# Encoder block on one core: a re-ordered front and a re-timed attention plan

## The chip, the cores and the metric

The kernel runs on one core of a Trainium2 chip. Five engines work side by side, each through its own queue in order: TensorE (PE in the profile; its weight loads are PEld), VectorE (DVE), ScalarE (ACT), GpSimd (POOL) and SyncE (SP), which issues nearly all DMAs. The metric is the device time of one execution in microseconds (us); the time of the kernel before is the median of three executions.

## The reference, cut to what matters

One encoder block on 512 tokens, preceded by 16 meta tokens (528 columns in all), with a model width of 1024.

```python
u = rms_norm(h, pre_mix_gain)
qa, ka, va, qb, kb, vb, g = split(u @ w_in)
qa, ka, qb, kb = (rope(t, pos) for t in (qa, ka, qb, kb))
o_swa = windowed_gqa_sink_attention(qa, ka, va, sink)       # 16 query heads on 4 key heads, width 64
lam = exp(sum(lq1 * lk1)) - exp(sum(lq2 * lk2)) + lambda_init
o_diff = differential_attention(qb, kb, vb, lam)            # 8 heads: (softmax(q1 k1) - lam softmax(q2 k2)) v
merged = sigmoid(g1) * (o_swa @ w_swa) + sigmoid(g2) * (o_diff @ w_diff)
h = h + rms_norm(merged @ w_out, post_mix_gain)
u = rms_norm(h, pre_ffn_gain)
h = h + rms_norm((silu(u @ w_gate) * (u @ w_up)) @ w_ffn_out, post_ffn_gain)
```

## The kernel before, in words

**Arithmetic.** Every operand of a large product is split into a high part (rounded to fp32r) and a low remainder, and a product is three matmuls, high by high, high by low, low by high (mm3, lines 286 to 288). ScalarE makes the high part, VectorE or GpSimd the low one (split at L256, sub_hi at L252). A weight tile is 128 x 1024 (0.5 MB): a raw tile "wr" (three buffers) is loaded, then split into "wh" and "wl" (three each). x is transposed in memory and kept as xh and xl, eight chunks of 128 rows by 528 columns, scaled by the norm's gain; the norm's own factor for each token, rbc, is multiplied in only after the products.

**The front** (L364 to about L500) is written out by hand. DVE, ACT and SP take its instructions in the order of the program, inside a block called start; PE takes the whole kernel so. In order:

- 60 warm-up matmuls on a zero tile (L377).
- The loads: vec (small vectors, the gain among them), chunk 0 of x, the first half of the two key weights wA and wB, the rest of x, the second halves after chunk 2. x_load and x_split (L388 to L395) load and split a chunk of x, w_half (L397 to L403) half a weight tile. Then load_w loads and splits wV (the first value weight) and wV2 (the second); its cast is L271. Then come the four tiles xn of plain x, xm (the meta tokens), ident and rot (the table of the rotation).
- The key products: for each of the eight chunks k, and for wA and wB, and for both halves of the 528 columns (HALF is 264), one mm3. Then the product of wV, into two banks pV.
- The norm: sums of squares of the five tiles, on ACT (L454, three of them) and DVE (L456, two). After them ACT copies the key sums out of PSUM (kraw, L461 and L462). rsqrt_cols makes the inverse root (POOL and DVE), and PE turns it into a row by five transposes (L468 and L471); ACT copies it into rbc (L472, L473).
- lambda: a DMA of its vectors into lt (L481), two reductions on DVE (L485), an exponential on ACT (L487), and two operations on DVE that leave -lambda in nlam (L488, L489).
- two masks and a zeroed tile.

**The attention plan.** From L502 the kernel does not issue instructions directly: it makes a list of some 2,580 tasks, each with an engine, an assumed cost, what it reads and writes, which ring of buffers it takes a place from, a priority, and for a DMA (land) how long the data takes after the issue. Plan.run (L175) goes through them like a small model of the chip, when the kernel is built: at each step it takes, of the engines' next possible tasks, the one that can start first; of those within 0.12 us of each other on one engine, the one with the earliest due time. For PE the due time is the priority itself, for the other engines the time at which the task is ready plus SLACK of its priority. The order that comes out is the fixed order of each engine's queue on the chip; the modelled times are not used there.

In the plan: the two value products of the windowed attention (v_swa; that of wV2 is made in the plan, by products, from the splits that the front made), transposed by PE after a scaling by rbc on DVE into VT (L581; transposes at L591 and L599); the rotation of the keys, copied by SP into place (move, L569); four groups of queries (q_swa, two weight tiles each, 512 columns), 16 blocks of windowed attention (s_swa, products at L706; t_swa, transposes at L755, products at L762 and L765); gate products; eight heads of differential attention (qk, vd, s_diff with products at L854, t_diff with products at L894 to L909); and branch products that fill in between. weights() loads and splits a weight tile for all of them (cast at L522); odd ones get their low part from POOL, even ones from DVE. s_diff multiplies by nlam for each head's second softmax (L872). Tag "vt" has one buffer, for VT.

The plan ends near 500 us. The second branch, the output product, the norm and the feed-forward part (to 951 us) follow in hand-written order.

Of the kernel before, what the change touches and what calls it, by code (L numbers as in the profile page):

```python
# [20 lines left out]
P = 128  # L21
# [94 lines left out]
class Plan:  # L116
# [6 lines left out]
    AFTER = dict(PE=0.22, ACT=0.07, DVE=0.07, POOL=0.12, SP=0.1)  # L123

    def __init__(self, tags):
        self.slots = {t: [0.0] * n for t, n in tags.items()}
        self.tasks, self.sigs, self.bufs, self.last = [], {}, [], {}
# [47 lines left out]
    def run(self):  # L175
        free = dict.fromkeys(("PE", "ACT", "DVE", "POOL", "SP"), 0.0)
# [3 lines left out]
        while any(todo.values()):  # L180
            best = None
            for e, ks in todo.items():
                cand = []
                for k in ks:
                    t = 0.0
                    for d in k.deps:
                        if d.done is None:
                            t = None
                            break
                        t = max(t, d.done + (0.0 if d.eng == e else self.AFTER[d.eng]))  # L190
# [5 lines left out]
                    for tag, n in need.items():  # L196
# [4 lines left out]
                        t = max(t, f[n - 1] + 0.07)  # L201
# [3 lines left out]
                    due = k.prio if e == "PE" else t + self.SLACK.get(k.prio, 6.0 + 0.002 * k.prio)  # L205
                    cand.append((max(t, free[e], port if k.port else 0.0), due, k))
# [18 lines left out]
            free[k.eng] = t + k.cost  # L225
            k.done = t + k.cost + k.land
            if k.port:
                port = t + k.cost
            k.fn()
            for b in k.bufs:  # L230
                b.left -= 1
                if not b.left and b.tag is not None:
                    self.slots[b.tag][b.slot] = max(u.done + (0.0 if u.eng == "PE" else 0.0) for u in b.users)
# [3 lines left out]
def encoder(ctx, tc, I, out, dbg=None):  # L237
# [209 lines left out]

    ss = const.tile([P, 5], F32, name="ss")
# [9 lines left out]
    kraw = [atp.tile([P, EXT], F32, tag="q", name="kraw", bufs=8) for _ in range(2)]  # L458
    for s in range(2):
        cs = slice(s * HALF, (s + 1) * HALF)  # L460
        act.copy(out=kraw[0][:, cs], in_=kA[s])  # L461
        act.copy(out=kraw[1][:, cs], in_=kB[s])  # L462
# [8 lines left out]
    pe.transpose(out=Sw[1][:, 0:P], in_=rb, identity=ident)  # L471
    act.copy(out=rbc[:, NMETA:EXT], in_=rps)  # L472
# [6 lines left out]

    lt = atp.tile([P, 4, 64], F32, tag="rt", name="lt", bufs=RT)  # L480
    sp.dma_start(out=lt, in_=I["lam"])  # L481
    lj = atp.tile([P, 2, 64], F32, tag="rt", name="lj", bufs=RT)
    ls = const.tile([P, 2], F32, name="ls")
    for c in range(2):
        dve.tensor_tensor_reduce(out=lj[:, c], in0=lt[:, 2 * c], in1=lt[:, 2 * c + 1], scale=1.0,  # L485
                                 scalar=0.0, op0=ALU.mult, op1=ALU.add, accum_out=ls[:, c:c + 1])
    act.activation(out=ls, in_=ls, func=AF.Exp)  # L487
    dve.tensor_tensor(out=nlam, in0=ls[:, 1:2], in1=ls[:, 0:1], op=ALU.subtract)  # L488
# [1097 lines left out]
```

## Time and profile before

| | |
|---|---|
| median of 3 runs | 949.91 us (949.45 to 951.23) |
| the profiled execution | 952.51 us |
| its span, first to last instruction | 950.7 us |
| TensorE busy | 932.1 us (98%) |
| VectorE, ScalarE, GpSimd busy | 716.5, 525.3, 216.7 us |
| mean granted TensorE clock | 0.996 |
| bytes moved by DMA | 110.46 MB, 116 GB/s in the mean |

The profile is of one execution. Times count from its first instruction. Rows of a timeline give the start, the duration, the engine, the line of the kernel, the operation, what it writes and reads, and in brackets how long the engine was idle before it and what released it. A row of the table by stretches gives the stretch, its length, the busy time and number of instructions of PE, PEld, DVE, ACT and POOL, the granted clock (1.00 is full), the DMA engines' busy share and GB/s. Rows of the groups give the line, the operation, its tiles and shape, the count, the busy time, the mean ns of one and the idle time before them. Rows of the waits give who waited for whom, the sum, how often, and the longest. The rows of the DMA issues end in the KB of each and the median us from issue to landing. Matmuls overlap in the array, so their durations add up to more than the time between their starts.

### The profile page before, as it was taken

The numbers are of one execution on the slowest core, as the hardware profiler recorded it, in microseconds if no ns is written. First come the engines' busy times: TensorE is split into PE (matmuls) and PEld (weight loads), VectorE is DVE, ScalarE is ACT, GpSimd is POOL, SyncE is SP. The second block draws the span as 40 slices with busy tenths as digits, with TensorE's granted clock in tenths as the row PEclk, the third lists the DMA queues.
The fourth block names the chain that finished last, engine by engine and source line by source line (L and its number), as shares of the span: only waits on it lengthen the run. The fifth ranks groups of instructions, "written<-read, shape, count | busy, mean of one in ns | idle before, by whom it ended". The sixth has DMA issues, their size and how long they took to land.

```text
span 950.7 us, 15639 instructions
## 1 busy us (share of the span) xinstructions
PE 932.1 (98%) x5871; PEld 833.9 (88%) x5871; DVE 716.5 (75%) x1230; ACT 525.3 (55%) x954; POOL 216.7 (23%) x228
## 2 busy tenths in 40 slices
PE   9899999999999999999999999999999999999996
PEld 9787888889898999989887888998999999988885
DVE  5747898999664658878773865885787887799975
ACT  6326776775644446667556443563555555565541
POOL 0544455543222423243211421400000000000000
PEclk9999999999999999999999999999999999999999
DMA  9483222251535144333531470354433333180122
GB/s 333 132 216 100 68 78 73 73 135 45 135 89 144 58 113 134 82 107 127 157 111 55 162 223 26 91 189 143 116 107 96 115 101 111 46 332 16 52 67 88
DMA packets 37579, 110.46 MB, mean 116 GB/s; under 512 B 6129, under 2 KB 6641, under 8 KB 37505
## 3 DMA queue, kind: packets, MB, share of 16 engines
q1 hardware_dynamic: 37504, 109.47, 38.4%
q8 instruction: 46, 0.75, 0.3%
q14 instruction: 29, 0.23, 0.1%
HBM read 88.09 MB, written 2.10 MB: 95 GB/s over the span
## 4 chain that ended last, share of the span: by engine, by line
PE 85%; DMA 5%; DVE 4%; ACT 2%; SPq 2%; issue 1%; POOL 1%; DVEq 0%; POOLq 0%; ACTq 0%
PE pr L286 19%; PE pr L288 19%; PE pr L287 19%; PE Sd L854 3%; PE wk L287 2%; PE wk L286 2%; PE wk L288 2%; PE Sw L706 2%; PE O L762 2%; PE tr L894 2%; PE Od L907 2%; DMA wr<-in_w_in_dram 2%; PE tr L755 2%; PE tr L287 1%; PE tr L288 1%; PE tr L286 1%
## 5 line engine op out<-in xcount | busy, mean ns | idle before, releaser
L286 PE MATMUL pr<-xh,wh 128*128 128x264 f32 (+1 forms) x616 | 200.6, 326 | 0.0
L287 PE MATMUL pr<-xl,wh 128*128 128x264 f32 (+1 forms) x616 | 196.9, 320 | 0.8 <-DVE xl L394 0.8
L288 PE MATMUL pr<-xh,wl 128*128 128x264 f32 (+1 forms) x616 | 196.8, 319 | 0.3 <-POOL wl L252 0.3
L252 POOL TENSOR_TENSOR wl<-wr,wh 128x1024 fp32r<-128x1024 f32 (+2 forms) x42 | 100.0, 2382 | 142.0 <-ACT wh L522 78.8
L288 PEld LDWEIGHTS pr<-xh,wl 128*128 128x128 f32 x616 | 116.3, 189 | 9.0 <-POOL wl L252 0.5
L287 PEld LDWEIGHTS pr<-xl,wh 128*128 128x128 f32 x616 | 116.5, 189 | 8.8 <-DVE xl L394 1.2
L286 PEld LDWEIGHTS pr<-xh,wh 128*128 128x128 f32 x616 | 116.2, 189 | 7.7 <-issue 0.2
L522 ACT CAST wh<-wr 128x1024 fp32r<-128x1024 f32 x56 | 58.5, 1048 | 45.0 <-PE pr L287 29.7
L252 DVE TENSOR_TENSOR wl<-wr,wh 128x1024 fp32r<-128x1024 f32 (+2 forms) x58 | 67.9, 1174 | 17.4 <-ACT wh L271 8.5
L308 POOL TENSOR_TENSOR r3y<-r3v,mhalf 128x1 f32<-128x1 f32 x4 | 2.2, 551 | 326.9 <-DVE r3v L307 326.9
L286 PE MATMUL pr<-TM,sx 128*128 128x256 f32 x236 | 66.9, 283 | 0.3 <-ACT s L1368 0.3
L287 PE MATMUL pr<-TM,sx 128*128 128x256 f32 x236 | 66.8, 283 | 0.0
L288 PE MATMUL pr<-TM,sx 128*128 128x256 f32 x236 | 66.8, 283 | 0.0
L859 DVE TENSOR_REDUCE nm<-Sd 128x1 f32<-128x528 f32 x64 | 45.1, 705 | 20.8 <-PE Sd L854 19.9
L252 DVE TENSOR_TENSOR sx<-S,sx 128x1024 fp32r<-128x1024 f32 x34 | 41.6, 1225 | 25.1 <-PE pr L287 12.7
L288 PE MATMUL pr<-uh,wl 128*128 128x256 f32 (+1 forms) x188 | 55.0, 292 | 0.4 <-DVE wl L252 0.4
L286 PE MATMUL pr<-uh,wh 128*128 128x256 f32 (+1 forms) x188 | 55.1, 293 | 0.0
L287 PE MATMUL pr<-ul,wh 128*128 128x256 f32 (+1 forms) x188 | 54.9, 292 | 0.0
L559 POOL TENSOR_TENSOR ta<-ta,tb 128x528 f32<-128x528 f32 (+1 forms) x26 | 36.4, 1400 | 79.8 <-DVE tb L547 53.9
L256 ACT CAST sx<-S 128x1024 fp32r<-128x1024 f32 x34 | 35.7, 1050 | 25.5 <-PE pr L288 9.2
L862 ACT ACTIVATE pp<-Sd,nm 128x528 f32<-128x528 f32 x40 | 28.0, 700 | 39.3 <-DVE pa L875 22.6
L720 POOL TENSOR_SCALAR p<-p,rc 128x272 f32<-128x272 f32 (+1 forms) x64 | 36.1, 577 | 48.4 <-DVE rc L718 45.1
(522 smaller groups left out, 2641.6 us busy)
## 6 DMA issues: line engine op xcount, KB each, us to landing
wr<-in_w_in_dram SPq DMA_DIRECT2D x50, 512.0 KB, 4.4
wg<-in_w_fi_dram SPq DMA_DIRECT2D x17, 512.0 KB, 3.6
wu<-in_w_fi_dram SPq DMA_DIRECT2D x17, 512.0 KB, 3.5
wr<-in_w_fi_dram SPq DMA_DIRECT2D x16, 512.0 KB, 4.3
b<-in_w_fo_dram SPq DMA_DIRECT2D x16, 512.0 KB, 8.7
Kd<-hl SPq DMA_DIRECT2D x32, 132.0 KB, 2.4
Kd<-Kd SPq DMA_DIRECT2D x16, 264.0 KB, 3.9
Q<-hl SPq DMA_DIRECT2D x64, 64.0 KB, 3.1
```

What stands on the lines that cost most here:

```text
L252: (eng or dve).tensor_tensor(out=lo, in0=src, in1=hi.bitcast(F32), op=ALU.subtract)
L256: act.copy(out=hi, in_=src)
L286: pe.matmul(out=ps, lhsT=ah, rhs=bh, start=first, stop=False, **more)
L287: pe.matmul(out=ps, lhsT=ah, rhs=bl, start=False, stop=False, **more)
L288: pe.matmul(out=ps, lhsT=al, rhs=bh, start=False, stop=last, **more)
L522: T("ACT", 1.05, lambda: act.copy(out=wh.t, in_=wr.t), r=[wr], w=[wh], prio=pr_)
L559: T("POOL", 0.05 + 1.3 * m, lambda: pool.tensor_tensor(out=ta.t[:, :, 0:n], in0=ta.t[:, :, 0:n], in1=tb.t[:, :, 0:n], op=ALU.add), r=[tb], ...
L706: pe.matmul(out=Sw2[S.slot][:, 0:nk], lhsT=QS[g][hh].t[:, i * P:(i + 1) * P], rhs=KB[g].t[:, x, r0:r1], start=(x == 0), stop=(x == 1))
L720: T("POOL", 0.2 + 0.43 * c, lambda z=z: pool.tensor_scalar(out=pt.t[:, z, 0:nk], in0=pt.t[:, z, 0:nk], scalar1=rc.t[:, z:z + 1], scalar2=1 ...
L854: pe.matmul(out=S.t[:, s, 0:HALF], lhsT=Q[c].t[:, i * P:(i + 1) * P], rhs=K[c].t[:, x, s * HALF:(s + 1) * HALF], start=(x == 0), stop=(x = ...
L859: T("DVE", 0.71, lambda S=S, c=c, one=one: dve.tensor_reduce(out=nm.t[:, c, one], in_=S.t[:, :, 0:HALF], axis=AX.XY, op=ALU.min), r=[S], w ...
L862: T("ACT", 0.9, lambda S=S, c=c, one=one, p=p: act.activation(out=p().rearrange("p (a b) -> p a b", a=2), in_=S.t[:, :, 0:HALF], func=AF.E ...
```

## The change

Four things are changed; the matmuls, their shapes and their number stay.

**First operands.** x chunk 0 is loaded first, then vec. The weight tiles wA and wB come in three pieces instead of two halves: chunks 0 and 1 after x chunk 0, chunks 2 and 3 after x chunk 1, chunks 4 to 7 after x chunk 3. In the key products of chunk 0 the twelve matmuls are put in another order: the four high by high first, then the four with xl, then the four with wl.

**Second V product.** wV2 is loaded and split after xn and xm instead of before them. The kraw copies move from behind the last sum of squares to behind the first. The product of wV2 is made in the front, in two banks of "pr": the first four chunks of its first half before the five transposes of the norm, the rest after them. The plan no longer holds it.

**lambda** moves into the plan as tasks, its DMA after the transposes of block 5, with lt in the "vt" buffer; the DVE multiply by nlam waits for it.

**The planner.** Its engines' ends, signal delays and costs are replaced by other figures, the engines start at given times (PE at 3.7), and the due times of 206 tasks are moved by the amounts of a list (SHIFT).

```diff
-    AFTER = dict(PE=0.22, ACT=0.07, DVE=0.07, POOL=0.12, SP=0.1)
+    OVER = dict(PE=0.0, ACT=0.098, DVE=0.083, POOL=0.03, SP=0.0)
+    DRAIN = dict(PE=0.165, ACT=0.0, DVE=0.0, POOL=0.0, SP=0.0)
+    def lag(a, b):
+        return 0.07 if b == "PE" else 0.06 if b == "SP" else 0.092 if b == "POOL" and a in ("ACT", "DVE") else 0.036
+    SHIFT = """
+        28:20 51:-25 66:6.4 98:5 111:6 146:7 155:8 175:-5 184:17 198:-4.3 216:-89 218:-15 222:-6 257:-68 266:0.7
...
+        2579:48"""
...
-                        t = max(t, d.done + (0.0 if d.eng == e else self.AFTER[d.eng]))
+                        t = max(t, d.start + d.cost if d.eng == e == "PE" else d.done + self.lag(d.eng, e))
...
                     due = k.prio if e == "PE" else t + self.SLACK.get(k.prio, 6.0 + 0.002 * k.prio)
+                    due += self.shift.get(k.n, 0.0)
...
-            free[k.eng] = t + k.cost
-            k.done = t + k.cost + k.land
+            free[k.eng] = t + max(0.06, k.cost - self.OVER[k.eng]) if k.eng != "PE" else t + k.cost
+            k.done = t + k.cost + k.land + self.DRAIN[k.eng]
...
-    x_load(0)
-    w_half(wA, 0, 0)
-    x_split(0)
-    w_half(wB, 1, 0)
-    for k in range(1, KT):
+    for k in range(KT):
         x_load(k)
         x_split(k)
-        if k == 2:
-            w_half(wA, 0, 1)
-            w_half(wB, 1, 1)
+        for k0, k1 in {0: ((0, 2),), 1: ((2, 4),), 3: ((4, KT),)}.get(k, ()):
+            w_part(wA, 0, k0, k1)
+            w_part(wB, 1, k0, k1)
     wA, wB = wA[1:], wB[1:]
     wV = load_w(I["w_in"][2], dst=[atp.tile([P, KT, P], F32R, tag="p", name="wV", bufs=2) for _ in range(2)])
-    wV2 = load_w(I["w_in"][3])
     for t in range(4):
         sp.dma_start(out=xn[:, t], in_=I["x"][t * P:(t + 1) * P])
     sp.dma_start(out=xm, in_=I["meta"])
+    wV2 = load_w(I["w_in"][3])
...
     for k in range(KT):
...
+        todo = [(ps_, w[a][:, k, :], (xh, xl)[b][:, k, cs], k == 0 and a == b == 0, k == KT - 1 and a == 1)
+                for hs, w in ((kA, wA), (kB, wB)) for ps_, cs in zip(hs, halves) for a, b in ((0, 0), (0, 1), (1, 0))]
+        if k == 0:
+            todo = [x for p in range(3) for x in todo[p::3]]
+        for ps_, a, b, first, last in todo:
+            pe.matmul(out=ps_, lhsT=a, rhs=b, start=first, stop=last)
...
+        if t == 0:
+            for ps_, raw in ((kA, kraw[0]), (kB, kraw[1])):
+                for s in range(2):
+                    act.copy(out=raw[:, halves[s]], in_=ps_[s])
+    pV2 = [pr_t(HALF), pr_t(HALF)]
+    def v2(h, ks):
+        for k in ks:
+            mm3(pV2[h], (wV2[0][:, k, :], wV2[1][:, k, :]), (xh[:, k, halves[h]], xl[:, k, halves[h]]), k == 0, k == KT - 1)
+    v2(0, range(KT // 2))
     rst = rsqrt_cols(const, ss, P, 1.0 / D, "r0")
...
     pe.transpose(out=Sw[1][:, 0:P], in_=rb, identity=ident)
+    v2(0, range(KT // 2, KT))
+    v2(1, range(KT))
...
-                   ta=2, tb=1, vt=1, rt=RT, ma=3))
+                   ta=2, tb=1, vt=1, rt=RT, ma=3), dict(PE=3.7, ACT=0.05, DVE=0.05, POOL=0.0, SP=0.0))
...
-          w=[wr], dep=dep, prio=pr_, land=3.6 if nfill[0] > 3 else 0.3)
+          w=[wr], dep=dep, prio=pr_, land=4.0 if nfill[0] > 3 else 0.0)
...
-            T("PE", 3 * mm_t(c1 - c0),
+            T("PE", 0.694 if c1 - c0 == NTOK else 0.367,
...
-    def move(out, in_, r, w, dep=(), land=2.7):
+    def move(out, in_, r, w, dep=(), land=2.3):
...
+    def lam_task():
+        lt = sb("vt", [P, 4, 64], F32, "lt", 1)
+        T("SP", 0.35, lambda: sp.dma_start(out=lt.t, in_=I["lam"]), w=[lt], dep=Ttr[5][-1:], prio=60, land=3.0)
...
-    v_swa([products(w3, X, X_, h * HALF, (h + 1) * HALF) for h in range(2)])
+    v_swa(PV2)
```

The other costs of the plan are changed in the same way, by up to a few tenths of a microsecond each (a transposition of four blocks from 0.50 to 0.355, an exponential of a differential head from 0.90 to 0.79, a low part on POOL from 2.65 to 2.42).

More of the change, by code (lines that the diff above doesn't have):

```diff
@@ L175, in run @@
     def run(self):
-        free = dict.fromkeys(("PE", "ACT", "DVE", "POOL", "SP"), 0.0)
+        free = self.free
         port = 0.0
@@ L232, in run @@
                 if not b.left and b.tag is not None:
-                    self.slots[b.tag][b.slot] = max(u.done + (0.0 if u.eng == "PE" else 0.0) for u in b.users)
+                    self.slots[b.tag][b.slot] = max(u.done for u in b.users)
         self.end = max(k.done for k in self.tasks)
@@ L445, in encoder @@
         proj(pV[h], wV, X, h * HALF, (h + 1) * HALF)
+    kraw = [atp.tile([P, EXT], F32, tag="q", name="kraw", bufs=8) for _ in range(2)]
     ss = const.tile([P, 5], F32, name="ss")
@@ L478, in encoder @@
     pool.tensor_scalar(out=g08, in0=vec[:, 40:41], scalar1=1.0 - LAMBDA_INIT, scalar2=1.0, op0=ALU.mult, op1=ALU.mult)
[L480 to L488, printed above, removed]
-    dve.tensor_scalar(out=nlam, in0=nlam, scalar1=-LAMBDA_INIT, scalar2=None, op0=ALU.add)
     bd1 = atp.tile([P, 512], F32R, tag="rt", name="bdm", bufs=RT)
@@ L572, in encoder @@
     X_ = []
-    w3 = [pl.held(t, x) for t, x in zip(("wh", "wl"), wV2)]
+    for t in ("wh", "wl"):
+        pl.slots[t][0] = 3.9
     def v_scaled(pv):
@@ L639, in encoder @@
     PV = [pl.held("tr", t) for t in pV]
+    PV2 = [pl.held("pr", t) for t in pV2]
     for b in MK:
@@ L696, in s_swa @@
         sm = [buf() for _ in range(2)]
-        T("POOL", 0.27, lambda: pool.tensor_copy(out=pt.t[:, :, nk], in_=nsink[:, 4 * g:4 * g + 4]),
+        T("POOL", 0.2, lambda: pool.tensor_copy(out=pt.t[:, :, nk], in_=nsink[:, 4 * g:4 * g + 4]),
           w=[pt] + ph, prio=0)
@@ L811, in qk @@
                      [hl], [K])
-            move(lambda K=K: K.t[64:128], lambda K=K: K.t[0:64], [], [K], land=4.0)
+            move(lambda K=K: K.t[64:128], lambda K=K: K.t[0:64], [], [K], land=3.6)
             for i in range(2):
@@ L861, in s_diff @@
                   prio=0)
-                T("ACT", 0.9, lambda S=S, c=c, one=one, p=p: act.activation(
+                T("ACT", 0.79, lambda S=S, c=c, one=one, p=p: act.activation(
                     out=p().rearrange("p (a b) -> p a b", a=2), in_=S.t[:, :, 0:HALF], func=AF.Exp, scale=-1.0,
@@ L867, in s_diff @@
                 if c == 0:
-                    T("POOL", 0.78, lambda p=p, one=one: pool.tensor_scalar(
+                    T("POOL", 0.715, lambda p=p, one=one: pool.tensor_scalar(
                         out=p(), in0=p(), scalar1=rc.t[:, 0, one], scalar2=1.0, op0=ALU.mult, op1=ALU.mult),
@@ L878, in s_diff @@
         hd["a"], hd["A"], hd["keep"] = a, A, [pa, pp[0]]
+    def lam_task():
+        lt = sb("vt", [P, 4, 64], F32, "lt", 1)
+        ls = const.tile([P, 2], F32, name="ls")
+        T("SP", 0.35, lambda: sp.dma_start(out=lt.t, in_=I["lam"]), w=[lt], dep=Ttr[5][-1:], prio=60, land=3.0)
+        LS = buf()
+        for c in range(2):
+            T("DVE", 0.23, lambda c=c: dve.tensor_tensor_reduce(
+                out=lt.t[:, 2 * c], in0=lt.t[:, 2 * c], in1=lt.t[:, 2 * c + 1], scale=1.0, scalar=0.0, op0=ALU.mult,
+                op1=ALU.add, accum_out=ls[:, c:c + 1]), w=[lt, LS], prio=7, port=True)
+        T("ACT", 0.2, lambda: act.activation(out=ls, in_=ls, func=AF.Exp), w=[LS], prio=7)
+        T("DVE", 0.16, lambda: dve.tensor_tensor(out=nlam, in0=ls[:, 1:2], in1=ls[:, 0:1], op=ALU.subtract),
+          w=[LS], prio=7)
+        T("DVE", 0.16, lambda: dve.tensor_scalar(out=nlam, in0=nlam, scalar1=-LAMBDA_INIT, scalar2=None, op0=ALU.add),
+          w=[LS], sig="lam", prio=7)
     lnx, dd, results, B1 = [], [], [], []
@@ L898, in t_diff @@
                 T("ACT", 0.58, lambda: act.copy(out=aTm[32:48, :], in_=tr.t[0:16, :]), r=[tr], w=[AM], prio=1)
-                hd["Av"].append(T("PE", mm_t(512), lambda: pe.matmul(out=O.t, lhsT=m.t, rhs=aTm, start=False, stop=True),
+                hd["Av"].append(T("PE", 0.232, lambda: pe.matmul(out=O.t, lhsT=m.t, rhs=aTm, start=False, stop=True),
                                   r=[AM, m], w=[O], prio=0))
@@ L990, in encoder @@
         T("ACT", 0.36, lambda c=c: act.copy(out=aTm[:, c * 256:(c + 1) * 256], in_=zero), w=[AM], prio=2)
+    lam_task()
     qk(0)
```

75 lines of the change are left out of this document (35 added, 40 removed), and 15 rows, old and new, of the table SHIFT.

## The prediction

> **What bounds the kernel now.** I read the page first, then the table by stretches of time, then TensorE's own waits, then the timelines around them.
>
> ```profile
> span 950.7 us, 15639 instructions
> ...
> PE 932.1 (98%) x5871; PEld 833.9 (88%) x5871; DVE 716.5 (75%) x1230; ACT 525.3 (55%) x954; POOL 216.7 (23%) x228
> ...
> PE 85%; DMA 5%; DVE 4%; ACT 2%; SPq 2%; issue 1%; POOL 1%; DVEq 0%; POOLq 0%; ACTq 0%
> ```
>
> ```profile
> 6.00:24.90 18.90, 18.07 (x146) 17.50 (x144) 12.66 (x19) 13.07 (x22) 0.61 (x1) 1.00 1.03 392
> 24.90:35.10 10.20, 8.98 (x67) 8.15 (x65) 7.93 (x20) 3.88 (x8) 5.80 (x7) 1.00 0.45 142
> 35.10:38.50 3.40, 1.06 (x7) 0.50 (x5) 3.37 (x8) 1.54 (x3) 2.38 (x2) 1.00 0.13 51
> 38.50:42.00 3.50, 3.50 (x11) 2.72 (x10) 3.10 (x4) 1.11 (x3) 3.50 (x3) 0.51 0.05 4
> 42.00:500.00 458.00, 453.69 (x2826) 400.70 (x2826) 344.60 (x742) 271.43 (x576) 167.26 (x177) 1.00 0.40 108
> ```
>
> TensorE is busy 98% of the span and carries 85% of the chain, so time is won only where it waits. Behind each stretch and its length stand the busy times of PE, PEld, DVE, ACT and POOL, then the granted clock, the DMA share and GB/s. The change touches only what lies before 500 us, and the matmuls stay the same in number. PE idles 1.22 us in 24.9 to 35.1, 2.34 in 35.1 to 38.5, and 4.31 in 42 to 500, where the attention plan rules; at 38.5 to 42 it is busy, but at clock 0.51.
>
> Busy time hides small waits, because matmuls overlap:
>
> ```profile
> 232.56 0.28 PE L287 MATMUL pr<-xl,wh 128*128 128x264 f32 x1
> 232.69 0.28 PE L288 MATMUL pr<-xh,wl 128*128 128x264 f32 x1
> 233.68 0.39 PE L854 MATMUL Sd<-Kd,Qd 128*128 128x264 f32 x1 [0.72 <-ACT pp L862]
> ...
> 506.27 0.40 PE L286 MATMUL pr<-xh,wh 128*128 128x512 f32 x1
> 506.50 0.40 PE L287 MATMUL pr<-xl,wh 128*128 128x512 f32 x1
> ```
>
> A 264-wide matmul reads 0.28 us but is followed after 0.12; a 512-wide one reads 0.40 and is followed after 0.23. The wait shown as 0.72 really cost 0.99 - 0.12 = 0.87, and waits under 0.16 are not shown at all. So I count the plan's work by shape:
>
> ```profile
> L286 PE MATMUL pr<-xh,wh 128*128 128x264 f32 x384 | 111.2, 290 | 0.0
> ...
> L286 PE MATMUL pr<-xh,wh 128*128 128x512 f32 x172 | 68.8, 400 | 0.0
> ...
> L854 PE MATMUL Sd<-Kd,Qd 128*128 128x264 f32 x256 | 43.3, 291 | 1.0 <-ACT pp L862 0.7
> ...
> L921 PE MATMUL mp<-sh,ones 128*128 128x512 f32 x7 | 2.8, 394 | 0.0
> ```
>
> In 42 to 500 there are 3 x 384 + 256 = 1408 matmuls of 264 columns (L287 and L288 are like L286) and, from the x172 row to the x7 row, 918 of 512. At 0.121 and 0.2325 that is 170 + 213 us. The other 500 of the 2826 (64 of 400 columns, 64 of 272, 372 transposes of 128) I put at 0.155 and 0.09, between those spacings and below: 53 us. Together 436 of 458, so about 22 us go into waits, of which the profile shows 4.3.
>
> **The change part by part.** The sum is made on the profiled execution, 952.51 us (span 950.7 and 1.8 around it), 2.6 above the median of 949.91; I carry the gain over to the median.
>
> *First operands.* The warm-up matmuls end where real work begins:
>
> ```profile
> 0.97 5.14 PE L377 MATMUL wps<-warm 128*128 128x128 bf16 x60 [0.97 <-DVE warm L374]
> ...
> 5.92 0.37 PE L286 MATMUL pr<-xh,wh 128*128 128x264 f32 x1
> ...
> 6.71 0.39 PE L287 MATMUL pr<-xl,wh 128*128 128x264 f32 x1 [0.42 <-DVE xl L394]
> ...
> 8.27 0.39 PE L286 MATMUL pr<-xh,wh 128*128 128x264 f32 x1
> ...
> 9.08 0.39 PE L287 MATMUL pr<-xl,wh 128*128 128x264 f32 x1 [0.41 <-DVE xl L394]
> ```
>
> They stay, so nothing starts before 5.9. What can go is 6.71 - 5.92 - 0.12 = 0.67 and 0.69 the second time. For k = 0 the four high-by-high matmuls now come first and cover the making of xl and wl: the first stall goes. The second, on x of k = 1 and 2, shrinks by little, because the loads run at a full DMA share (1.03 in 6 to 24.9). I take 0.8, between 0 and 1.4.
>
> *The norm chain.* This is where I expect the price of the new front.
>
> ```profile
> 16.67 1.05 ACT L271 CAST wh<-wr 128x1024 fp32r<-128x1024 f32 x1
> 18.01 1.06 ACT L454 ACTIVATE jk<-xn 128x1024 bf16<-128x1024 f32 x1 [0.29 <-DMA xn<-in_x_dram]
> ...
> 22.85 1.06 ACT L454 ACTIVATE jk<-xm 16x1024 bf16<-16x1024 f32 x1 [0.73 <-DMA xm<-in_meta_dram]
> 23.81 0.18 ACT L454 ACTIVATION_READ_ACCUMULATOR jk<-xm 16x1 f32 x1
> 23.91 0.35 ACT L461 COPY kraw<-pr 128x264 f32<-128x264 f32 x1
> ...
> 26.44 0.69 PE L468 MATMUL rps<-ident,rb 128*128 128x128 f32 x4 [1.21 <-issue]
> ```
>
> On ScalarE this part runs in program order: the kraw copies stand behind the last Square although their sums were long ready. The second V weight's cast (L271) still stands ahead of the first Square, but its 0.5 MB now queues behind xn and xm. With the DMA engines full, the same bytes are ahead of its end as of xm's end now, so I put its landing at 22.3 (xm's is 22.8; x now leads the queue, half a microsecond sooner). Then follow one cast, a Square, four kraw copies of 0.35 that overlap a little, two Squares: 22.3 + 1.0 + 1.1 + 1.1 + 1.15 + 1.15 = about 27.6. VectorE's subtraction and two reductions run beside them. From the last accumulator read (23.99) to the first transpose (26.44) it takes 2.45 us, so that comes at 30.0, 3.5 later. The 12 V2 matmuls put ahead as filler last 12 x 0.12 = 1.45 and wait for the first kraw copy (24.8): TensorE idles from 26.3 to 30.0, 3.7 us where it idles 1.4 now. Bounds: no delay if the weight lands as early as the first xn (18.0), 4 us if it trails xm.
>
> *The clock.* In the stretch 35.1 to 38.5 TensorE worked 1.06 us, and the stretch after it was granted 0.51:
>
> ```profile
> 36.16 0.33 PE L599 MATMUL tr<-ident,VT 128*128 128x128 f32 x1 [0.69 <-DVE VT L581]
> 38.14 0.57 PE L599 MATMUL tr<-ident,VT 128*128 128x128 f32 x3 [1.65 <-DVE VT L581]
> 38.44 0.70 PE L286 MATMUL pr<-xh,wh 128*128 128x512 f32 x1
> 38.94 0.63 PE L287 MATMUL pr<-xl,wh 128*128 128x512 f32 x1
> 39.36 0.63 PE L288 MATMUL pr<-xh,wl 128*128 128x512 f32 x1
> ...
> 42.06 0.40 PE L288 MATMUL pr<-xh,wl 128*128 128x512 f32 x1
> ```
>
> Matmuls came 0.42 apart instead of 0.23; nine of them from 38.44 to 42.29 lost 1.7 us. My new idle of 3.7 should bring the same, partly over idle time: 1.2, between 0 and 1.7. [...]
>
> *Second V product and lambda.* Those two VT waits (and the lost clock) go, since V2 is done before the plan and VectorE is rid of lambda ahead of it:
>
> ```profile
> 30.92 1.78 DVE L485 CUSTOM_DVE_ANT_0 lj<-lt 128x64 f32<-128x64 f32 x1 [0.57 <-DMA lt<-in_lam_dram]
> ...
> 36.03 0.91 DVE L488 TENSOR_TENSOR nlam<-ls 128x1 f32<-128x1 f32 x1
> ```
>
> Moved into the plan, lambda is one DMA issue on SP after the transposes of block 5, four small VectorE operations, one on ScalarE, and a wait for head 0's first multiply by nlam; it borrows the vt tile that V of head 0 needs next. VectorE has 458 - 344.6 us free there: nothing, or 2.7 us (1.78 + 0.91) if it stretches again with head 0 behind it. The transposes of V2 are covered by the query products; without cover they cost the 1.65 of today.
>
> To one common point (V2 done, ten V transposes, 15 query matmuls) the trace takes 42.06 + 0.23 = 42.3. After: 30.0 + 0.6 (five transposes) + 36 x 0.12 + 1.2 + 0.9 + 15 x 0.232 = 40.5. **Front: 1.8 us won**, the 0.8 above being lost in the idle.
>
> *The plan.* No task is added but lambda's; the order on five queues changes, PSUM and weight slots included. What it can win:
>
> ```profile
> PE Sw L706 <- DMA Q<-hl: 1.1, 1, 1.1
> PE Sd L854 <- ACT pp L862: 0.7, 1, 0.7
> ...
> PE tr L755 <- DVE al L252: 0.2, 1, 0.2
> ```
>
> Eight such waits sum to 3.7, with 0.16 hidden in each 5.0. Leaving out the DMA's 1.25, a better order can take 3.7; of the 17 unseen I take 15%, 2.5, because most are likelier signalling than order. **Plan: 6.2 won**, between -4.4 (below) and all 22. Sum 8.0: 944.5 on the profiled execution, 941.9 on the median.
>
> **The rivals.** *The norm chain is not late*: the weight lands early, or ScalarE takes the Squares first. Then the transposes come at 26.3 right behind the filler, 3.7 and the 1.2 of clock are won too: 941.9 - 4.9 = 937.0. Against it: program order and the full DMA share. *The plan changes nothing*: PE's losses are signalling, not order; 949.9 - 1.8 = 948.1. For it: only 4.3 of 22 are shown. *The new order trusts operands too soon*, the slower case:
>
> ```profile
> Q<-hl SPq DMA_DIRECT2D x64, 64.0 KB, 3.1
> ```
>
> The plan now books 0.6 + 2.3 = 2.9 us for a move; these take 3.1. If the first product of each of the four query groups waits as the one above did (1.1), that is 4.4 lost against 1.8: 952.5. It decides from two such waits on; against it: the whole plan now shows one such wait.
>
> **How the numbers follow.** Forecast 0.58, norm chain early 0.20, plan neutral 0.12, operands late 0.10. A measurement of this kernel tells about 0.2%, 1.9 us. Faster: the forecast but for a tail, and the first rival, 0.78; same: the neutral plan and the tail, 0.13; slower 0.09. The range, 935 to 949, takes in the front's bounds (0 to 6.7) and most of the plan's.
>
> **What would show it.** Right: Squares behind the V2 cast near 23, an idle of over 3 us before L468 with a clock near 0.5 after it, no wait on VT, the plan's window 6 us shorter. Wrong: L468 near 26, a shown idle in the plan over 4.3, or new waits on Q moves.

## The result and the profile after

The changed kernel takes **964.25 us** (median of 4 runs, 961.62 to 966.69); the kernel before, beside it, 950.57 (4 runs, 949.45 to 951.94). The ratio is 1.0138, 95% interval 1.0123 to 1.0153: slower by about 13.7 us, where 8.0 less was forecast, and outside the range. The profiled execution took 962.16 us, 2.1 below its median, and that of the kernel before 952.51, 1.9 above its median, so the two profiles show 9.65 us of the 13.7.

From the page of the profile after, the span and the first row of busy times:

```profile
span 960.3 us, 15643 instructions
...
PE 933.7 (97%) x5871; PEld 834.0 (87%) x5871; DVE 727.6 (76%) x1232; ACT 523.6 (55%) x956; POOL 220.2 (23%) x228
```

TensorE has the same 5871 matmuls and about the same busy time; the 9.6 us of span that it is longer are waits and half clock. The table by stretches of the profile after (same columns as in the prediction) says where:

```profile
6.00:24.90 18.90, 18.46 (x152) 17.94 (x149) 9.35 (x14) 9.84 (x15) 0.01 (x1) 1.00 0.99 371
24.90:35.10 10.20, 6.14 (x48) 5.96 (x49) 7.24 (x19) 5.88 (x14) 6.00 (x7) 1.00 0.37 122
...
42.00:440.00 398.00, 393.36 (x2495) 348.72 (x2494) 309.87 (x668) 232.95 (x509) 153.31 (x166) 1.00 0.39 107
440.00:540.00 100.00, 93.35 (x465) 77.18 (x464) 64.34 (x104) 55.57 (x96) 26.11 (x16) 0.97 0.31 92
```

and the last two stretches of the profile before:

```profile
42.00:440.00 398.00, 393.79 (x2488) 349.24 (x2487) 300.28 (x660) 234.95 (x508) 151.01 (x165) 1.00 0.39 106
440.00:540.00 100.00, 99.91 (x517) 83.88 (x516) 67.22 (x110) 57.45 (x97) 28.61 (x18) 1.00 0.38 113
```

From 42 to 440 us the new order is neither better nor worse (2495 instructions against 2488). From 440 to 540 it does 465 instead of 517: 52 matmuls fewer, most of them one per 0.23 us, are nearly all of the loss in the profile, with 6.6 us of idle and a mean clock of 0.97. TensorE's waits after:

```profile
PE rps L501 <- issue: 3.6, 1, 3.6
PE Sd L879 <- DMA wr<-in_w_in_dram: 2.6, 1, 2.6
PE pr L313 <- ACT dh L984: 2.5, 1, 2.5
PE tr L623 <- DVE VT L605: 1.7, 1, 1.7
PE tr L615 <- POOL vr L613: 1.3, 1, 1.3
```

Before, the wait of the first row was 1.2 us, and no wait on dh, on vr or on a load for the scores was in the list. The second and third lie between 440 and 540; the fourth, on VT, lies at 423.7 us, in the stretch whose sum did not change. **The wait for 2.6 us** is at head 7; TensorE's timeline after:

```profile
472.55 0.27 PE L934 MATMUL tr<-ident,pp 128*16 128x128 f32 x1
475.47 0.73 PE L879 MATMUL Sd<-Kd,Qd 128*128 128x264 f32 x4 [2.65 <-DMA wr<-in_w_in_dram]
```

and the stretch behind it:

```profile
476.10:479.50 3.40, 3.40 (x10) 2.62 (x10) 1.55 (x3) 1.37 (x3) 0.70 (x1) 0.51 0.05 17
```

The scores of head 7 wait for their operands, and the next 3.4 us run at half clock. The releaser named is a weight load, but scores read no weight. SP's queue of the same run (SPq, the issues of DMAs) shows what is behind it:

```profile
461.26 1.03 SPq L543 DMA_DIRECT2D wr<-in_w_in_dram  x2
462.35 0.54 SPq L592 DMA_DIRECT2D Qd<-hl  x1
462.94 1.29 SPq L592 DMA_DIRECT2D Kd<-hl  x2
464.28 1.33 SPq L592 DMA_DIRECT2D Qd<-hl  x2
468.15 1.14 SPq L592 DMA_DIRECT2D Kd<-Kd  x2
...
471.31 0.54 SPq L592 DMA_DIRECT2D Qd<-hl  x1
```

and before, at the same place, with TensorE's scores behind them:

```profile
456.96 0.59 SPq L569 DMA_DIRECT2D Qd<-hl  x1
457.60 1.08 SPq L520 DMA_DIRECT2D wr<-in_w_in_dram  x2
458.78 0.51 SPq L569 DMA_DIRECT2D Kd<-Kd  x1
...
467.22 0.73 PE L854 MATMUL Sd<-Kd,Qd 128*128 128x264 f32 x4
```

Head 7's operands are made by eight moves out of hl, then two copies Kd<-Kd that need the key moves landed, then the last Qd moves. In both runs two gate weights of 0.5 MB stand among them, and what is issued behind these lands late. Before, they stood behind all eight moves: the copies could be issued at once, and the last operand of the first scores landed at 467.13, 0.1 us ahead of them (467.22). The copies and moves behind the weights took 5.2 to 6.7 us there too, so this place was on the edge already, though no wait was listed. After, they stand behind the third move (459.20 to 460.58). By the trace they landed at 465.32 and 467.12, and the Qd and Kd moves issued at 462.35 and 462.94 only behind them, at 467.42 and 468.08, where a move of Qd takes 2.1 us in the median of before. So the copies were issued at 468.15 only, and the last Qd that the first scores need landed at 475.27, 0.2 us ahead of them.

**The wait for 2.5 us** is behind the plan, where the second branch needs head 7's result dh:

```profile
514.38 0.40 PE L939 MATMUL Od<-aTm,Vdm 128*128 128x512 f32 x1
...
530.68 0.76 PE L313 MATMUL pr<-dh,wh 128*128 128x512 f32 x1 [2.45 <-ACT dh L984]
```

The 3.4 us behind it are at half clock:

```profile
530.80:534.20 3.40, 3.40 (x8) 2.35 (x9) 1.49 (x3) 1.68 (x2) 0.84 (x1) 0.51 0.03 5
```

and before:

```profile
504.64 0.39 PE L899 MATMUL Od<-aTm,Vdm 128*128 128x512 f32 x1
...
513.01 0.40 PE L286 MATMUL pr<-dh,wh 128*128 128x512 f32 x1
```

The last product of head 7 comes at 514.38, only 4.2 us ahead of the branch's first product (518.55), which reads the first seven heads; before there were 8.4 us of cover, and no wait on dh. The first product of the branch is 5.5 us later than before, the last matmul of the kernel 9.7 (952.50 against 942.84).

**The front** did the first steps as forecast. ScalarE after:

```profile
22.97 1.05 ACT L298 CAST wh<-wr 128x1024 fp32r<-128x1024 f32 x1 [5.94 <-DMA wr<-in_w_in_dram]
23.93 1.05 ACT L481 ACTIVATE jk<-xn 128x1024 bf16<-128x1024 f32 x1
```

and TensorE:

```profile
30.68 0.69 PE L501 MATMUL rps<-ident,rb 128*128 128x128 f32 x4 [3.57 <-issue]
...
40.09 0.33 PE L615 MATMUL tr<-ident,vr 128*128 128x128 f32 x1 [1.31 <-POOL vr L613]
...
41.85 0.40 PE L315 MATMUL pr<-xh,wl 128*128 128x512 f32 x1
```

The fifteenth query product ends its step at 41.85 + 0.23 = 42.08 us, against 42.3 before.

### The profile page after: what moved, and what is told of

It is laid out like the page before. It is cut to its first block, busy times and chain, and to the rows that moved or that the text cites. A ratio compares the mean times of both kernels' runs of the same rounds, so it can differ in the third digit from the quotient of the medians.

```text
span 960.3 us, 15643 instructions
## 1 busy us (share of the span) xinstructions
PE 933.7 (97%) x5871; PEld 834.0 (87%) x5871; DVE 727.6 (76%) x1232; ACT 523.6 (55%) x956; POOL 220.2 (23%) x228
## 4 chain that ended last, share of the span: by engine, by line
PE 81%; DVE 8%; ACT 4%; DMA 3%; issue 2%; SPq 1%; POOL 0%; DVEq 0%; POOLq 0%; ACTq 0%
PE pr L313 18%; PE pr L315 18%; PE pr L314 18%; PE Sd L879 3%; DMA wr<-in_w_in_dram 3%; PE wk L314 2%; PE wk L313 2%; PE wk L315 2%; PE tr L934 2%; PE O L787 2%; PE tr L780 2%; PE Sw L731 2%; PE Od L947 1%; PE tr L315 1%; PE tr L313 1%
## 5 line engine op out<-in xcount | busy, mean ns | idle before, releaser
L313 PE MATMUL pr<-xh,wh 128*128 128x264 f32 (+1 forms) x592 | 193.8, 327 | 0.9 <-ACT kraw L488 0.5
L315 PE MATMUL pr<-xh,wl 128*128 128x264 f32 (+1 forms) x592 | 190.1, 321 | 0.4 <-DVE wl L279 0.3
L314 PE MATMUL pr<-xl,wh 128*128 128x264 f32 (+1 forms) x592 | 190.1, 321 | 0.0
L315 PEld LDWEIGHTS pr<-xh,wl 128*128 128x128 f32 x592 | 111.8, 189 | 9.7 <-DVE wl L279 0.7
L313 PEld LDWEIGHTS pr<-xh,wh 128*128 128x128 f32 x592 | 111.7, 189 | 8.2 <-ACT kraw L488 0.7
L314 PEld LDWEIGHTS pr<-xl,wh 128*128 128x128 f32 x592 | 111.9, 189 | 7.3
L279 DVE TENSOR_TENSOR wl<-wr,wh 128x1024 fp32r<-128x1024 f32 (+2 forms) x60 | 71.9, 1201 | 16.1 <-ACT wh L298 14.5
L279 DVE TENSOR_TENSOR sx<-S,sx 128x1024 fp32r<-128x1024 f32 x34 | 41.6, 1224 | 24.9 <-PE pr L314 12.7
L879 PE MATMUL Sd<-Kd,Qd 128*128 128x264 f32 x256 | 44.2, 294 | 3.8 <-DMA wr<-in_w_in_dram 2.6
```

Of the source, the lines that this page charges most:

```text
L279: (eng or dve).tensor_tensor(out=lo, in0=src, in1=hi.bitcast(F32), op=ALU.subtract)
L313: pe.matmul(out=ps, lhsT=ah, rhs=bh, start=first, stop=False, **more)
L314: pe.matmul(out=ps, lhsT=ah, rhs=bl, start=False, stop=False, **more)
L315: pe.matmul(out=ps, lhsT=al, rhs=bh, start=False, stop=last, **more)
L879: pe.matmul(out=S.t[:, s, 0:HALF], lhsT=Q[c].t[:, i * P:(i + 1) * P], rhs=K[c].t[:, x, s * HALF:(s + 1) * HALF], start=(x == 0), stop=(x = ...
```

## The experiments

Ratios are to the kernel before on the same chip, with their 95% interval. "Old planner" means the old costs and delays, "new planner" the new ones. The "plan's own idle" is TensorE's idle time in the planner's bookkeeping while the kernel is built; no chip time. Three theories run through the expectations: that the shifted due times make the loss (S); that the old, too large costs of TensorE kept a reserve which the new ones lack (P); and that the old order is a favourable draw, so that any change of the numbers loses (J). "The first label" in the expectations of e7 and e9 is e6.

The kernel before, run beside each group of runs, had medians of 950.57 to 952.11 us. So a difference of medians can be off by up to 1.5 us where the runs stood on different chips; the ratios take that out, and differences are given by them where it matters.

| run | order | plan's own idle | median us | ratio |
|---|---|---|---|---|
| changed kernel | new planner, shifts | 1.3 | 964.25 | 1.0138 [1.0123, 1.0153] |
| e1_no_shift | new planner, no shifts | 5.8 | 964.11 | 1.0119 [1.0099, 1.0138] |
| e3_v2_first | changed, V2 weight first | 1.3 | 961.44 | 1.0103 [1.0081, 1.0124] |
| e4_front_only | old planner, new front | 7.7 | 953.11 | 1.0012 [1.0003, 1.0022] |
| e5_moves_first | changed, moves first | 1.4 | 958.71 | 1.0073 [1.0055, 1.0092] |
| e6_old_plan_v2_first | e4, V2 weight first | 7.7 | 950.62 | 0.9983 [0.9968, 0.9999] |
| e7_exact_pe_costs | e6, new TensorE costs | 22.9 | 962.56 | 1.011 [1.0083, 1.0138] |
| e8_no_shift_padded | e3, no shifts, padded | 5.7 | 973.94 | 1.0224 [1.0199, 1.0249] |
| e9_jitter | e6, costs within 3% | 8.0 | 956.28 | 1.0038 [1.0022, 1.0053] |
| e10_vt_moved | e6, two instructions moved | 7.7 | 948.95 | 0.9973 [0.9962, 0.9984] |
| e11_jitter_b | e6, costs within 3% | 11.1 | 958.61 | 1.0073 [1.006, 1.0086] |
| e12_jitter_new | e3, costs within 3% | 14.6 | 990.99 | 1.041 [1.0392, 1.0428] |
| e13_moves_and_v2 | e3 and e5 | 1.4 | 954.32 | 1.0027 [1.0015, 1.0039] |
| e14_side_costs | e6, new side costs | 6.6 | 975.14 | 1.026 [1.0243, 1.0277] |
| e15_landings | e6, new DMA landings | 10.2 | 964.15 | 1.0144 [1.0126, 1.0163] |
| e16_new_plan_old_landings | e3, no shifts, old move landings | 6.8 | 957.21 | 1.0064 [1.0049, 1.0079] |
| e17_cover_last_head | e13, more cover for dh | 1.4 | 954.46 | 1.0032 [1.0019, 1.0045] |

**e1_no_shift.** The list of shifted due times is emptied.

```diff
-    SHIFT = """ ... """
+    SHIFT = ""
```

> The changed kernel with an empty list of shifts; front, costs and lambda stay. Theory S (the 206 shifts pack the plan so tightly that head 7's operand moves come just in time and land late): the waits of 2.6 us on the moves of head 7 and of 2.5 us on the last dh go, with the clock halvings behind them, and the median falls from 964 to about 954. Rival C (the measured durations themselves, without slack, do it): the same waits stay and the median stays within 3 us of 964. Rival F (the front does it): also within 3 us of 964, with the waits of the end shorter.

964.11 us, as the changed kernel. The shifts move the places of the waits; the sum stays within the two intervals. The waits on dh and on the weight are gone, and others stand there:

```profile
PE rps L484 <- issue: 3.6, 1, 3.6
PE tr L763 <- DVE bdm L754: 2.4, 1, 2.4
PE Sd L862 <- DMA Qd<-hl: 1.8, 2, 1.0
```

That the shifts alone make the loss is refuted. In this run SP has all eight moves of head 7 ahead of the weights again (460.49 to 465.17, weights at 465.86), with the same booked landings.

**e4_front_only.** The kernel before with the new front, V2 in the front and lambda in the plan; the old planner, with TensorE starting at 3.7. The plan's list of tasks is another by that, and from 73 us on so is its order.

> The kernel before with the new front, the second V product in the front and lambda in the plan, but with the old planner: old costs, no shifts (only TensorE's start at 3.7 is kept). Theory S: the front is about neutral (42.1 against 42.3 us at the sixteenth 512-wide product), so 948 to 953. Rival F: 958 or more, as the front carries the loss.

953.11 us. With the old planner the new front costs 0.12% (0.03 to 0.22) instead of winning 1.8 us; how much of that is the front itself and how much the other order behind it is not shown. The new planner, by the ratios of e4 and the changed kernel, costs about 12. TensorE's wait and the stretch behind it, in e4:

```profile
31.06 0.66 PE L474 MATMUL rps<-ident,rb 128*128 128x128 f32 x2 [3.56 <-issue]
```

```profile
29.40:36.20 6.80, 5.14 (x24) 5.17 (x25) 4.56 (x12) 1.75 (x4) 4.26 (x5) 0.50 0.22 65
```

The half clock that the prediction put behind this idle is here, over 6.8 us.

**e3_v2_first** and **e6_old_plan_v2_first.** The V2 weight is loaded ahead of xn again: in the changed kernel (e3) and in e4 (e6).

```diff
     wV = load_w(I["w_in"][2], ...)
+    wV2 = load_w(I["w_in"][3])
...
     sp.dma_start(out=xm, in_=I["meta"])
-    wV2 = load_w(I["w_in"][3])
```

> The changed kernel with the second V weight loaded and split ahead of xn, as before. Rival F (the late norm chain is the main loss): the first norm transpose comes at about 26 us instead of 30.7 and the median falls by 8 us or more, to 956 or less. Theory S: the transpose comes 4 us sooner, but a part of that is given back at the next wait (the POOL copy of V2); the median falls by 2 to 4 us, to 960 to 962, and the waits of 2.6 and 2.5 us at the end stay.

> The front-only kernel (old planner) with the second V weight ahead of xn. All theories: no idle of 3.7 us before the norm transposes and no halved clock after it, so 3 to 5 us below the front-only kernel: 948 to 950, against 952 of the kernel before on this chip.

961.44 and 950.62 us: the place of the load is worth 2.8 and 2.5 us by the medians (3.3 and 2.8 by the ratios), under either planner, and the order of the plan is the same with and without it. The two intervals touch with the new planner and are apart with the old; e6 lies 0.6 us above its band. The first transposes in e3 come 3.7 us sooner than in the changed kernel:

```profile
26.99 0.69 PE L501 MATMUL rps<-ident,rb 128*128 128x128 f32 x4 [0.30 <-PE pr L315]
```

In e6 the two VT waits, which should have gone with V2 in the front, are still there, and what follows them:

```profile
31.49 2.78 DVE L543 TENSOR_TENSOR ta<-kraw,rot 128x528 f32<-128x528 f32 x1
34.19 0.70 DVE L543 TENSOR_TENSOR tb<-kraw,rot 128x528 f32<-128x528 f32 x1
...
36.71 2.83 DVE L543 TENSOR_TENSOR tb<-kraw,rot 128x528 f32<-128x528 f32 x1
39.47 0.42 DVE L578 TENSOR_TENSOR VT<-pr,rbc 128x264 f32<-128x264 f32 x1
```

```profile
36.90:40.30 3.40, 0.60 (x5) 0.41 (x5) 3.40 (x3) 0.58 (x2) 3.40 (x3) 1.00 0.14 16
40.30:43.70 3.40, 3.40 (x11) 2.62 (x10) 2.97 (x3) 0.90 (x2) 0.67 (x1) 0.50 0.36 140
```

**e5_moves_first.** The last four gate weights are issued only after head 7's last move.

```diff
-    gate2((0, 1, 2, 3), "hl", 1, S6[7:8], [heads[7]["moved"]])
+    gate2((0, 1, 2, 3), "hl", 1, [S6[7], heads[7]["moved"]], [heads[7]["moved"]])
```

> The changed kernel with one more dependency: the four last gate weights (0.5 MB each) are issued only after the last operand move of head 7, so that no weight stands between these moves in SP's queue. The rest of the plan's order stays nearly the same. Theory S with the DMA queue as its place: the moves land in 2 to 4 us as elsewhere, the wait of 2.6 us at head 7 and the halved clock behind it go; median 957 to 960, and 955 if the wait on dh shrinks too. Rival (the moves are late because the rotation before them is late, not because of the weights): the wait stays over 2 us and the median within 1.5 us of 964.

958.71 us, 5.5 less (6.2 by the ratios). SP's queue now has three weights behind the last move, the moves of Qd land in 2.0 us in the median, and head 7's wait is gone from the list:

```profile
470.02 2.57 SPq L592 DMA_DIRECT2D Qd<-hl  x3
472.64 1.55 SPq L543 DMA_DIRECT2D wr<-in_w_in_dram  x3
```

```profile
DMA to landing us min/median/max: 2.0/2.0/3.4
```

Up to 460 us all engines have the order of the changed kernel, and behind it some 50 instructions of about 8,700 stand elsewhere. So the loads among the moves are shown as a cause.

**e13_moves_and_v2.** Both edits, of e3 and e5, in the changed kernel.

> The changed kernel with the edits of e3_v2_first and e5_moves_first together: second V weight ahead of the xn load, and the last four gate weights issued behind head 7's moves. Alone they were worth 2.8 us (961.44 us) and 5.5 us (958.71 us). Theory (two separate waits in two stages, no common cause): they add, 955 to 957 us, and the rest above the old planner with the same front (950.62 us) stays unexplained by these two places. Rival (the order behind head 7 only hands the wait on): 958 to 961 us.

954.32 us, just under the band: they add (by the ratios 7.2 below e3, 10.6 below the changed kernel). The branch's first product comes at 511.69, with the old order of e6 at 510.99: with these two places mended the new plan is in the profiles as long as the old, no shorter. Behind it the wait on dh stays:

```profile
523.11 0.49 PE L313 MATMUL pr<-dh,wh 128*128 128x512 f32 x1 [1.73 <-ACT dh L984]
```

**e17_cover_last_head.** e13 with three columns of the second branch started ahead of dh.

```diff
-    first = [(load_w(I["w_bd"][j]), pr_t()) for j in range(2)]
+    first = [(load_w(I["w_bd"][j]), pr_t()) for j in range(3)]
```

> e13_moves_and_v2 (954.32 us) with one edit behind the plan: three columns of the second branch instead of two are multiplied by the first seven heads before the eighth is needed (21 more 512-wide matmuls, about 4.9 us, ahead of the first use of the last dh); the plan is the same. Theory 'last head late' (the wait of 1.7 us on dh and what follows it make most of the 3.7 us): the wait goes, 951 to 953 us. Rival (the 3.7 us lie elsewhere, or the third weight comes late and makes a wait of its own): 953.5 to 956 us.

954.46 us. The wait on dh is gone from TensorE's list, and from the branch's first product to the last matmul it takes 430.9 us (514.00 to 944.91) instead of 432.4. But the median did not fall, and the plan of the profiled run took 2.3 us longer, with the plan's order the same as in e13. So much can two executions of one order differ, and a difference of that size between two profiles shows nothing. Inconclusive: whether the last head's lateness costs time is not shown.

**e7_exact_pe_costs, e14_side_costs, e15_landings.** Each puts one group of the new numbers alone into e6: TensorE's costs; durations and delays of the other engines; landings of the DMAs.

e7, with the other TensorE costs likewise:

```diff
-            T("PE", 0.5, trans, ...)
+            T("PE", 0.355, trans, ...)
```

> As the kernel of the first label, but with TensorE's new costs (a transposition of four blocks 0.355 for 0.50, a score product 0.486 for 0.614, and so on); the other engines' costs, lags and landings stay old. Theory P (the old costs of TensorE held a reserve of some 25 us that paced the plan as the chip does, and the exact ones take it away): 5 to 10 us slower than the first label, 954 to 958. Rival E (the other engines' costs and signal lags took the reserve): within 2 us of the first label. Rival J (the old order is one good draw among many, and any change of costs loses it): slower as well.

e14, with the durations of VectorE, ScalarE and GpSimd:

```diff
-    AFTER = dict(PE=0.22, ACT=0.07, DVE=0.07, POOL=0.12, SP=0.1)
+    OVER = dict(...); DRAIN = dict(...); lag(a, b)
```

> e6_old_plan_v2_first (950.62 us: old planner, V2 weight first) with only the new durations and lags of VectorE, ScalarE and GpSimd and the new lag rules; TensorE's costs and the DMA landings stay old. The plan's own TensorE idle is 6.6 us (e6: 7.7). Theory 'reserve' (the new numbers for side engines and lags leave no room for what the chip adds, so waits appear): 956 to 965 us, with waits on ScalarE, VectorE and GpSimd. Rival 'TensorE's costs alone' (e7_exact_pe_costs lost 12 us, the side costs are only more exact): 949 to 953 us.

e15, with the key moves from 4.0 to 3.6 and the weights from 3.6 to 4.0:

```diff
-    def move(out, in_, r, w, dep=(), land=2.7):
+    def move(out, in_, r, w, dep=(), land=2.3):
```

> e6_old_plan_v2_first with only the new DMA landings in the plan: operand moves 2.7 to 2.3 us, key moves 4.0 to 3.6, weights 3.6 to 4.0 and 0 for the first three. The plan's own TensorE idle is 10.2 us (e6: 7.7). Theory 'landings' (moves that are planned to land in 2.3 us and land in 4 to 5 behind two 0.5 MB weights make the waits): 956 to 965 us with waits on Q, Qd, Kd or weights. Rival (any change of a number draws another order): 951 to 959 us, with waits mostly elsewhere; no loss at all would be 949 to 952 us.

962.56, 975.14 and 964.15 us: each group alone loses as much as all together, or more; e7 and e14 lie above the bands that their expectations give in numbers. None of the three is harmless, so none alone carries the loss. But each is one draw of the order, and how much of its loss comes from its numbers, and how much from any other order (J), is not shown. e15 is in the band of its theory, yet the largest sums of TensorE's waits in e7 and e15 are on ScalarE (10.4 and 7.4 us on pp; 0.7 before), not on moves. e14 loses at a granted clock of 1.00 in the plan's stretch from 42 to 500 us (0.998 in the mean of the run):

```profile
42.00:500.00 458.00, 443.05 (x2715) 380.40 (x2714) 342.03 (x725) 263.49 (x565) 163.96 (x175) 1.00 0.38 103
```

2715 instructions where the kernel before did 2826.

**e16_new_plan_old_landings.** The new planner without shifts, V2 weight first, the moves' landings at 2.7 and 4.0.

> The new planner without its shifted due times, V2 weight first, and the operand moves' landings as in the old planner (2.7 and 4.0 us instead of 2.3 and 3.6). The plan's own TensorE idle is 6.8 us (5.8 with the short landings). Theory 'landings': the waits on moves go, 951 to 955 us. Rival 'TensorE's and the side costs carry it': 958 to 968 us, with other waits in place of those on moves.

957.21 us, between the bands of the two theories; waits on a move stay, one of Q for 3.2 us the longest. Inconclusive.

**e8_no_shift_padded.** e3 without shifts, and 0.08 us added to TensorE's transposes and score products in the plan.

> The changed planner without shifts, V2 weight first, and 0.08 us added to the costs of the transpositions and score products of the attention on TensorE; everything else as measured. Theory P: the reserve is back for a good part, so 950 to 955 where 961 would come without it. Rival E and rival J: 958 or more.

973.94 us: more reserve in the plan did not bring less waiting. The theory that the old, too large costs of TensorE were a useful reserve misses its band of 950 to 955 by 19 us, on one draw of the order; it misses its band in e9 as well, by 2.7.

**e9_jitter, e11_jitter_b, e12_jitter_new.** Every cost of the plan times a fixed random number.

```diff
+        cost *= 1 + 0.03 * self.rng.uniform(-1, 1)
         k = Task(len(self.tasks), eng, cost, fn, ...)
```

> As the first label, but every cost of the plan is multiplied by its own random factor between 0.97 and 1.03 (one fixed draw): the same reserve, another order. Theory P: within 3 us of the first label. Rival J: 5 us or more slower.

> e6_old_plan_v2_first with every cost of the plan multiplied by another fixed random number between 0.97 and 1.03 (a second draw beside e9_jitter, 956.28 us). Theory J (any new set of numbers is a new draw of the order, and the old order is a good one): slower than e6 by 2 to 10 us, 953 to 961 us, with waits at other places than in e9. Rival (the old numbers do not matter within 3%, e9 was an unlucky draw): 950 to 952 us.

> e3_v2_first (new planner with its shifted due times, V2 weight first, 961.44 us) with every cost of the plan multiplied by a fixed random number between 0.97 and 1.03. The planner's own idle time for TensorE goes from 1.4 to 14.6 us. Theory J (the planner's fitted order is worth nothing on the chip beyond any draw): 955 to 967 us, no slower than e3 by more than the scatter of draws. Rival (the fit of 206 due times is worth its modelled 13 us on the chip): 970 to 976 us.

956.28 and 958.61 us on the old planner, 5.7 and 8.0 more than e6, by noise alone. In e9, with none of the new numbers, weights stand among head 7's moves too, and its scores wait 2.3 us. On the new planner 990.99, 30 more than e3: the theory that the fitted new order is worth no more than any draw fails on this one draw, the rival's band is even exceeded. The clock was at half in five places of e12; its longest drop:

```profile
244.50:251.30 6.80, 6.04 (x19) 5.09 (x20) 5.22 (x14) 2.43 (x7) 0.00 (x0) 0.50 0.75 195
```

**e10_vt_moved.** The order of e6, and by hand the two scalings of the second V (VT) ahead of the second half of the key rotation on VectorE. Every other instruction keeps its place. Tasks 34 and 35 are taken out of the finished order and put ahead of task 8.

```diff
+        pl.early, pl.ahead = pl.tasks[34:36], pl.tasks[8]
         pl.run()
```

> The kernel e6_old_plan_v2_first (950.62 us, old planner, V2 weight first) with two instructions of VectorE moved by hand in the finished order: the two scalings of the second V (VT <- pr, rbc) stand ahead of the second half of the key rotation (ta <- kraw, rot) instead of behind it; nothing else of the order changes on any engine. In e6 the transposes waited 0.5 and 2.8 us for them (36.8 and 39.95 us), behind a rotation stretched from 0.70 to 2.83 us, and the clock was at half from 40.3 to 43.7 us. Theory 'single waits make the time' (what the plan loses on the chip is a handful of waits of this kind, each with its half clock): both waits and the half clock go, 3.3 + 1.7 = 5 us, some of it taken again by the next waits: 945.0 to 947.5 us, faster than both kernels. Rival 'the in-order queues hand a wait on' (a wait removed here comes back at the next operand): 949.5 to 951 us, with the sum of PE's stalls unchanged at about 29 us.

948.95 us, 0.27% faster than the kernel before (0.16 to 0.38), the best of all; e6 without the edit is 0.17% faster (0.01 to 0.32). The wait of 2.8 us and the half clock are gone; VectorE's timeline:

```profile
34.09 0.76 DVE L585 TENSOR_TENSOR VT<-pr,rbc 128x264 f32<-128x264 f32 x2
...
36.92 2.03 DVE L550 TENSOR_TENSOR tb<-kraw,rot 128x528 f32<-128x528 f32 x1
```

and the stretch that was at half clock:

```profile
40.30:43.70 3.40, 3.40 (x15) 2.51 (x14) 3.30 (x6) 1.59 (x2) 0.55 (x1) 1.00 0.51 151
```

The rotation still stretches, but TensorE no longer waits for it. In the profiles the branch's first product comes 3.5 us sooner than in e6 (507.44, 510.99); the medians differ by 1.7, and the intervals overlap, so that e10 is faster than e6 is not shown. It lies between the two bands of the expectation.

## Why the prediction was wrong, point by point

*First operands.* Right: in the first 20 us TensorE's delays, counted from start to start over the usual spacing of each shape, fall from 1.68 to 0.97 us, 0.7 won of 0.8 forecast, and lost again in the idle behind it.

*The norm chain.* Right, as the rows above show: V2's weight landed at 22.95 (forecast 22.3), the first transposes came at 30.68 (30.0), the idle was 3.57 (3.7). (The terms of that sum add up to 27.8, not 27.6.) What it is worth, 2.5 to 3.3 us, is shown by e3 and e6; the rival "not late" had put it at 4.9.

*The clock.* In the profiled run the term was missing (clock 1.00 from 24.9 to 35.1), in e1 and e4 it came, 0.50 over 3.4 and over 6.8 us. So the step held in two of these three profiles; why it failed in this one is not shown. What one drop costs there was not measured by itself.

*Second V product and lambda.* Lambda cost nothing: its reductions took 0.22 us each at 144 us, and nobody waited for them. The two VT waits of 0.69 and 1.65 went, but the wait on vr (1.31) took their place, behind a rotation stretched to 2.78 us. **Front: 0.2 won in the profile, not 1.8**, and that only because the clock term of 1.2 did not come: without it the forecast for the common point was 39.3 us, and 42.08 was measured. The first transposes came 0.7 late, the wait on vr cost 1.5 with its hidden part, and the rest is small. With the old planner and this front e4 loses 0.12%.

*The plan.* This is the step that failed: "Plan: 6.2 won", between -4.4 and all 22. With the front the same, the new planner loses 11 to 12 us (e4 against the changed kernel, e6 against e3, by the ratios). The prediction's own sign of being wrong came: TensorE's shown idle from 42 to 500 us is 7.95 us, not under 4.3. My working took waits off one by one, as if nothing came instead. The 22 us of waits were also too many: at the median spacings of before, 0.18 us for 400 columns, 0.126 for 272, 0.10 in the mean for a transposition, the 500 other matmuls take 57 us, not 53, and about 18 are left.

From 42 to 440 us what the new order wins and what it loses come to nought in the profile; behind 440 two new waits, at places that had none, with a clock of 0.51 behind each, cost more than the bound; the second of them lies at 530 us, behind the 500 us at which the prediction let the change end. The rival "operands too soon" named the kind of wait, an operand's move that lands late, but put it at the four query groups at 1.1 us each, by the one wait shown; it was at head 7, where weights queue between the moves, and cost 5.5 to 7.2 us (e5, e13). That the booked 2.3 us are behind it is not shown: e1 books the same and has the weights behind all eight moves, e9 books the old 2.7 and has them among the eight. No wait of the profile before named that place, but its queue did: moves of 5.2 to 6.7 us, with 0.1 us in hand. That queue order is part of a re-planned order, and the working should have priced it.

*What is settled and what not.* By the ratios the loss is 13.1 us. About 3.3 of it are the V2 weight behind xn and 7.2 the weights among head 7's moves, both shown by undoing them. 2.6 stay (e13 against the kernel before, 1.4 to 3.7); the late last head is only a candidate. Why no new set of numbers gave an order better than the old one is open. The plan's own idle does not tell it: 1.3 us went with 964 us, 7.7 with 950.6, 6.6 with 975.

## What to carry to other kernels

An order from a planner is fixed at build time, but on the chip its waits come where the planner books nothing. It books a fixed landing for a move, whatever stands ahead of it in SP's queue, and it keeps marked tasks of VectorE and GpSimd apart, but the two products of a rotation on VectorE bear no such mark, and in e6 one of them took 2.83 us beside a subtraction on GpSimd, 0.70 alone. So judge a re-planned order on the chip, and do not sum the waits of the old profile as its gain: any change of a cost, 3% of noise too, moves all the orders behind it. Moving two named instructions in a finished order (e10) kept the rest and removed the wait that it aimed at; with e6, on which it stands, it is the only run under the kernel before.

## What the runs showed of the hardware that was not expected

**The clock.** An idle of 2.65 us at head 7 was followed by half clock (0.51), one of 3.57 in the front of the same run was not (1.00). In e1 the same 3.57 was (0.50); the stretches around it, after:

```profile
25.70:30.60 4.90, 1.41 (x12) 1.20 (x10) 2.96 (x11) 4.42 (x8) 1.96 (x2) 1.00 0.37 117
30.60:34.40 3.80, 3.72 (x31) 3.75 (x32) 2.82 (x7) 0.66 (x2) 2.54 (x4) 1.00 0.35 111
```

and in e1:

```profile
31.00:34.40 3.40, 3.40 (x18) 3.40 (x17) 2.19 (x5) 0.66 (x2) 2.25 (x4) 0.50 0.38 81
```

Each half clock that the stretches above show lasts 3.4 us, or 6.8 (in e4, and the longest of e12). The length of the idle alone does not tell whether one follows: behind 3.57 us the clock was 1.00 in the changed kernel and 0.50 in e1, behind 2.65 and 2.45 it was 0.51. What decides is not shown.

**VectorE beside GpSimd.** A rotation on VectorE (128x528, two operands) takes 0.70 us alone and 2.83 beside GpSimd's subtraction; that is what made VT late in e6. There the subtraction ran from 36.64 to 38.98, and the rotation, started at 36.71, ended at 39.54, 0.56 behind it. In the changed kernel a rotation took 2.78 us beside the subtraction that ran from 32.86 to 36.83, and ended at 37.40; the one behind it, at 37.33, took 0.70. Why a rotation takes longer there is not shown.
